# First norm's modulation: near halves as one-column TensorE products, far halves split over the engines

## The chip, the cores and the metric

The kernel runs on one core of a Trainium2 chip. The metric is device time of one execution in microseconds; the time of a kernel is the median of its runs. The engines are named as the profile does: PE (TensorE; PEld is its weight load), DVE (VectorE), ACT (ScalarE), POOL (GpSimd) and SP (SyncE, which issues nearly all DMAs).

## The reference, cut to what matters

```python
c_act = jax.nn.silu(c)
mod = c_act @ ada_w[l] + ada_b[l]                       # (1, 6*1024); ada_w is 1024 x 6144, f32
sh1, sc1, g1, sh2, sc2, g2 = [m[:, None, :] for m in jnp.split(mod, N_MOD, axis=-1)]
h = rmsnorm(x, norm_mix_w[l]) * (1.0 + sc1) + sh1       # x is 2048 x 1024
proj = h @ w_in[l]
...
x = x + g1 * mix
h = rmsnorm(x, norm_mlp_w[l]) * (1.0 + sc2) + sh2
```

Everything behind `proj` (a gated linear recurrence, sparse attention with a top-k indexer, a convolution module, the output product and a large MLP) fills the rest of the time; the change doesn't touch it. What it touches is the product of the vector `c_act` with the columns of `ada_w` that give `sc1` and `sh1`, 1024 columns each. No product with `w_in` can begin before the first columns of both are known.

## The kernel before

The sequence is cut into four blocks of 512 positions. For each block `in_block` normalizes x (`in_norm`), transposes it on PE into eight tiles of 128 channels, and applies scale and shift per channel while it splits each tile in a high part `ah` and a low part `al` (`to_act_steps`, L266: ACT makes `tf`, DVE makes `ah`, DVE or POOL makes `al`). Each unit of `w_in` then takes 24 PE products of 512 columns (three for each of eight channel tiles, `mm_T`, L357). Weights come in through SP's queue (`fetch_w`, `next_w`), are split by ACT (`whi`, L256) and POOL (`wlo`, L264), and the two parts are written back to DRAM for later blocks (`wk_d`).

Scale (`a1`) and shift (`sh1`) are made in four halves by `ada_half` (L207), 512 columns each, in this order: the first ("near") half of `a1` and of `sh1` at the kernel's start, L1677 and L1678, and the second ("far") halves in `first_units` (L1041), after the first two units have taken the products of channel tiles 0 to 3. Each half loads eight tiles `adw` of 128 rows x 512 columns, 256 KB each. Row tile k belongs to the column `cact[:, k]` of the activated c. For k = 1 and 2 ACT multiplies the tile by it (L224) and POOL adds the two (L227); for the other six DVE multiplies and accumulates (L229, L231). At the end `part_sum` sums the two folded tiles over the 128 partitions: PE takes 128 columns of the tile as stationary operand and a column of ones as moving operand, four such products for a tile, and each shows as two instructions (f32), all at L217. DVE then adds `ada_b` (L235) and, for `a1`, the norm's weight (L238).

The other four parts of the modulation come from `ada_gen` (L700), a side stream that the kernel pulls in small steps from the second block on: its parts (L183) load tiles of 128 x 256 (L186) into two buffers and accumulate on DVE (L188, L190).

The small constants (`ada_b`, the norms' weights and others) come as rows into the tile `rows` and are transposed once on PE to `cols` (L177, L178).

What sets the order: a scheduler works on a simulated time line when the program is built. It gives each engine its instructions in a fixed order, and takes first, of what is ready in its simulation, what stands earlier in the program; so work may run well ahead of its place in the program. Buffers belong to a pool and a tag, with a fixed number for each tag: "tf" (two buffers) holds the row of c, `rows`, the dumps of `in_norm`, and `tf` of `to_act_steps`. PSUM tiles go by tag as well. `S_st[h]` is the state of the recurrence of head h, which is cleared at the start and updated at the end of each head in each block (L680).

Of the kernel before, what the change touches and what calls it, by code (L numbers as in the profile page):

```python
# [8 lines left out]
F32 = mybir.dt.float32  # L9
# [7 lines left out]
OP = mybir.AluOpType  # L17
# [3 lines left out]
P = 128  # L21
D = 1024
L = 2048
TB = 512
NB = L // TB
NK = D // P
# [18 lines left out]
AK = [1, 2]  # L45
# [15 lines left out]
WQ, AQ, AB = 0, 0, 2  # L61
# [16 lines left out]
def trunk(ctx, tc, x, c, ada_w, ada_b, norm_mix_w, norm_mlp_w, w_in, hg_lb_logits,  # L78
# [3 lines left out]
    V, A, G, T = nc.vector, nc.scalar, nc.gpsimd, nc.tensor  # L82
# [11 lines left out]
    xp = ctx.enter_context(tc.tile_pool(name="xio", bufs=1))  # L94
# [19 lines left out]
    def ps_ax():  # L114
        return px["p"].tile([P, 512], F32, tag="ax", bufs=px["ax"], name=nm("ax"))
# [43 lines left out]
    pt = ps_ax()  # L159
# [13 lines left out]
        offs[key] = r0  # L173
        r0 += n
    cols = cst.tile([P, NROW], F32, name="cols")
    pt = ps_ax()
    T.transpose(pt[:, :NROW], rows, ident[:NROW, :NROW])  # L177
    V.tensor_copy(cols, pt[:, :NROW])  # L178

    def col(key, i=0, n=1):  # L180
        return cols[:, offs[key] + i:offs[key] + i + n]

    def ada_part(pool, wtag, wbufs, acc, sec, c0, w):  # L183
        for k in range(NK):
            t = pool.tile([P, w], F32, tag=wtag, bufs=wbufs, name=nm("adw"))
            (nc.gpsimd if AQ else nc.sync).dma_start(t, ada2[k * P:(k + 1) * P, sec * D + c0:sec * D + c0 + w])  # L186
            if k == 0:
                V.tensor_scalar(acc, t, cact[:, 0:1], None, op0=OP.mult)  # L188
            else:
                V.scalar_tensor_tensor(acc, t, cact[:, k:k + 1], acc, op0=OP.mult, op1=OP.add)  # L190
            yield 1.2 * w
# [12 lines left out]
    a2 = cst.tile([P, NK], F32, name="a2")  # L204
    g_d = {2: dram([1, D], F32, "g1_d"), 5: dram([1, D], F32, "g2_d")}

    def ada_half(sec, c0, dst, key, slots):  # L207
        acc = hp.tile([P, TB], F32, tag="cu", bufs=2, name=nm("adacc"))
        pt = ps_ax()
        n = TB // P  # L210
        t0 = c0 // P

        side = []

        def part_sum(t, vec, first, last):
            for i in range(n):
                T.matmul(pt[:, i:i + 1], t[:, i * P:(i + 1) * P], vec, start=(first and i == 0),  # L217
                         stop=last, skip_group_check=True)

        for k in range(NK):  # L220
            t = slots[k]()
            dma(t, ada2[k * P:(k + 1) * P, sec * D + c0:sec * D + c0 + TB])
            if k in AK:
                A.mul(t, t, cact[:, k:k + 1])  # L224
                side.append(t)
                if len(side) > 1:
                    G.tensor_tensor(side[0], side[0], t, OP.add)  # L227
            elif k == 0:
                V.tensor_scalar(acc, t, cact[:, 0:1], None, op0=OP.mult)  # L229
            else:  # L230
                V.scalar_tensor_tensor(acc, t, cact[:, k:k + 1], acc, op0=OP.mult, op1=OP.add)  # L231
        if side:
            part_sum(side[0], ones[:, 0:1], True, False)
        part_sum(acc, ones[:, 0:1], not side, True)
        V.tensor_tensor(dst[:, t0:t0 + n], pt[:, :n], col("adab", sec * 8 + t0, n), OP.add)  # L235
        if key is not None:
            part = slice(c0 // P, (c0 + TB) // P)
            V.scalar_tensor_tensor(dst[:, part], dst[:, part], 1.0, cols[:, offs[key] + part.start:offs[key] + part.stop],  # L238
                                   op0=OP.add, op1=OP.mult)
# [458 lines left out]
    AW = 256  # L698

    def ada_gen():  # L700
        for sec, dst in ((2, None), (4, a2), (3, sh2), (5, None)):
            for c0 in range(0, D, AW):
                acc = hp.tile([P, AW], F32, tag="ada", bufs=1, name=nm("adacc"))
                yield from ada_part(hp, "adw", AB, acc, sec, c0, AW)
                if dst is None:
                    pt = ps_xp(13)
                    T.matmul(pt[:1, :AW], ones, acc, start=True, stop=True)
                    row = hp.tile([1, AW], F32, tag="adw", bufs=AB, name=nm("adrow"))
                    dma(row, ada_b[0:1, sec * D + c0:sec * D + c0 + AW])
                    V.tensor_tensor(row, pt[0:1, :AW], row, OP.add)  # L710
                    dma(g_d[sec][:, c0:c0 + AW], row)
                else:
                    ada_col(acc, sec, c0, AW, dst)
            if sec == 4:
                ada_scale(a2, "nmlp")
# [325 lines left out]
    def first_units(xts):  # L1041
        act = [], []
        steps = to_act_steps(xts, a1, sh1, *act)
        ws = []
        for k in range(NK // 2):
            next(steps)
        for u in range(KO):
            ws.append(next_w())
            early.append(ps_at())
            mm_T(early[u], ws[u], act, True, None, 0, NK // 2)  # L1050
        ada_half(1, TB, a1, "nmix", far)
        ada_half(0, TB, sh1, None, far2)
        for _ in steps:
            pass
        for u in range(KO):
            mm_T(early[u], ws[u], act, True, None, NK // 2, NK)
        return act
# [616 lines left out]
    far2 = [slot("f", ZB), slot("k", ZB), slot("q", ZB), slot("v", VB), slot("gate", GB)]  # L1674
    far2 += [slot("at", 2), slot("at", 2), slot("u", 2)]
    xq = [in_norm(0)]
    ada_half(1, 0, a1, "nmix", near)  # L1677
    ada_half(0, 0, sh1, None, near)  # L1678
    while len(fetched) < NPF:
        sp = specs.pop(0)  # L1680
        fetched.append((fetch_w(*sp), sp))
# [73 lines left out]
```

## Time and profile before

| | us |
|---|---|
| median of 3 runs | 3005.93 |
| lowest, highest | 3005.49, 3018.01 |
| the profiled execution | 3011.41 |
| its span in the trace | 3009.7 |

The profile shows one execution, the profiled one; the other 1.7 us of its time lie around the span. All durations in this document are from that execution, while the comparison between kernels goes by the medians of runs. An engine's instructions run in their order; "idle before" a row is the time for which the engine stood, and the arrow names what ended it. PE's records of 512 columns overlap, so the distance of two starts, not the duration of one, is what a product costs in a stream.

### The profile page before, as it was taken

How to read it: one execution, taken by the hardware profiler on the slowest of the kernel's cores; microseconds unless marked ns; L12 is line 12 of the kernel's file. 1: busy time of each engine (PE TensorE's matmuls, PEld its weight loads, DVE VectorE, ACT ScalarE, POOL GpSimd, SP SyncE). 2: the span in 40 equal slices, each digit the busy share in tenths (PEclk: the TensorE clock that was granted, in tenths of full speed). 3: DMA queues.
4: the chain of work that ended last, by engine and by line, in shares of the span. 5: the costliest groups of instructions: out<-in, count | busy, mean ns of one | idle time of the engine just before them, and what ended most of it. 6: DMA issues, size and time to landing. Idle time of an engine off the chain costs nothing. (4 is left out here: it accounts for less than half of the span.)

```text
span 3009.7 us, 50821 instructions
## 1 busy us (share of the span) xinstructions
PE 2809.9 (93%) x18352; PEld 2539.2 (84%) x18352; DVE 1997.2 (66%) x3673; ACT 1545.7 (51%) x2885; POOL 1787.0 (59%) x1530
## 2 busy tenths in 40 slices
PE   6889989897999989999999999999989999989997
PEld 5768868786887888989898989998788899889997
DVE  7796486868437352766669566576988731487787
ACT  3436454445424235456566656466555544466654
POOL 7565152225305165566688666578766766867775
PEclk9999989998999999999999999999999999999999
DMA  8867756675665433444557545354899974465543
GB/s 265 275 195 249 222 175 219 197 216 187 202 195 168 137 121 129 120 127 140 148 165 228 155 137 148 100 179 153 256 295 313 305 237 141 147 207 178 178 124 110
DMA packets 479416, 560.10 MB, mean 186 GB/s; under 512 B 32615, under 2 KB 371884, under 8 KB 479148
## 3 DMA queue, kind: packets, MB, share of 16 engines
q1 hardware_dynamic: 478992, 556.65, 59.0%
q8 instruction: 145, 2.38, 0.3%
q14 instruction: 123, 1.01, 0.1%
q10 hardware_dynamic: 156, 0.07, 0.0%
HBM read 458.30 MB, written 98.31 MB: 185 GB/s over the span
## 5 line engine op out<-in xcount | busy, mean ns | idle before, releaser
L264 POOL TENSOR_TENSOR wlo<-wraw,whi 128x512 fp32r<-128x512 f32 x514 | 713.9, 1410 | 418.6 <-ACT whi L256 263.3
L256 ACT CAST whi<-wraw 128x1024 fp32r<-128x1024 f32 x257 | 269.7, 1050 | 335.8 <-PE ax L1172 105.8
L759 DVE SCALAR_TENSOR_TENSOR s<-r,iw_s,s 128x512 f32<-128x512 f32 (+3 forms) x266 | 267.3, 1005 | 193.6 <-ACT r L754 190.3
L357 PE MATMUL mm<-ah,wk 128*128 128x512 f32 x1104 | 296.9, 404 | 12.0 <-ACT k L577 3.3
L1172 PE MATMUL ax<-whi,hh 128*128 128x256 f32 x1600 | 278.9, 286 | 19.9 <-DVE acc L1334 13.1
L1172 PE MATMUL ax<-wlo,hh 128*128 128x256 f32 x1600 | 280.0, 285 | 0.0
L1172 PE MATMUL ax<-whi,hl 128*128 128x256 f32 x1600 | 275.8, 285 | 2.0 <-POOL hl L264 2.0
L941 POOL TENSOR_TENSOR pT<-L,pT 128x512 fp32r<-128x512 f32 (+3 forms) x160 | 201.5, 1261 | 123.7 <-ACT pT L940 104.7
L357 PE MATMUL mm<-ah,whi 128*128 128x512 f32 x936 | 256.4, 400 | 11.9 <-DVE gate L600 4.2
L357 PE MATMUL mm<-al,whi 128*128 128x512 f32 x936 | 257.1, 397 | 0.0
L1172 PEld LDWEIGHTS ax<-whi,hh 128*128 128x128 f32 x1600 | 232.1, 190 | 28.0 <-DVE acc L1334 12.9
L357 PEld LDWEIGHTS mm<-ah,wk 128*128 128x128 f32 x1104 | 207.2, 192 | 57.2 <-ACT k L577 4.0
L357 PE MATMUL mm<-ah,wlo 128*128 128x512 f32 x936 | 252.8, 394 | 0.0
L754 ACT ACTIVATE r<-ix 128x512 f32<-128x512 f32 (+3 forms) x256 | 141.4, 552 | 183.7 <-PE ix L752 177.3
L1172 PEld LDWEIGHTS ax<-wlo,hh 128*128 128x128 f32 x1600 | 232.2, 190 | 2.8
L1172 PEld LDWEIGHTS ax<-whi,hl 128*128 128x128 f32 x1600 | 229.7, 190 | 4.6 <-POOL hl L264 2.7
L528 POOL TENSOR_TENSOR cside<-cside,ctap 128x512 f32<-128x512 f32 x112 | 158.6, 1416 | 122.3 <-ACT ctap L527 105.8
L357 PEld LDWEIGHTS mm<-ah,whi 128*128 128x128 f32 x936 | 174.6, 191 | 49.5 <-DVE slo L470 4.9
L357 PEld LDWEIGHTS mm<-ah,wlo 128*128 128x128 f32 x936 | 175.2, 189 | 36.5
L357 PEld LDWEIGHTS mm<-al,whi 128*128 128x128 f32 x936 | 174.9, 190 | 35.1
L861 DVE TENSOR_SCALAR_CACHE_REDUCE cum<-s,ssm 128x384 bf16<-128x384 f32 (+13 forms) x112 | 165.3, 1475 | 6.5 <-POOL s L763 4.3
L1334 DVE TENSOR_TENSOR acc<-acc,ax 128x512 f32<-128x512 f32 x160 | 108.9, 682 | 84.9 <-PE ax L1172 84.5
(551 smaller groups left out, 6898.2 us busy)
## 6 DMA issues: line engine op xcount, KB each, us to landing
wraw<-in_mlp_w_dram SPq DMA_DIRECT2D x192, 512.0 KB, 4.1
wk<-wk_d SPq DMA_DIRECT2D x174, 512.0 KB, 4.9
kc<-sk_d SPq DMA_DIRECT2D x112, 256.0 KB, 3.8
vc<-v_d SPq DMA_DIRECT2D x112, 256.0 KB, 3.3
tsr<-in_mlp_w_dram SPq DMA_DIRECT2D x96, 256.0 KB, 5.8
ts_d<-tsr SPq DMA_DIRECT2D x48, 512.0 KB, 5.8
wr<-in_mlp_w_dram SPq DMA_DIRECT2D x96, 256.0 KB, 3.8
wr<-ts_d SPq DMA_DIRECT2D x72, 256.0 KB, 4.9
```

What stands on the lines that cost most here:

```text
L256: A.copy(hi, src)
L264: e.tensor_tensor(lo[:, i:j], src[:, i:j], hi[:, i:j].bitcast(F32), OP.subtract)
L357: T.matmul(ps, ww[:, k, :], aa[k], start=(n == 0 and k0 == 0), stop=(n == len(order) - 1 and k1 == NK))
L528: G.tensor_tensor(side, side, tap, OP.add)
L754: A.activation(r[:, :w], ps[:, :w], AF.Relu, scale=32.0 ** -0.5)
L759: V.scalar_tensor_tensor(s[:, c0:c0 + w], r[:, :w], iw, s[:, c0:c0 + w], op0=OP.mult, op1=OP.add)
L861: V.tensor_scalar(dump, s, t, -AIM - i * STEP, op0=OP.is_ge, op1=OP.add, accum_out=d)
L941: G.tensor_tensor(pT[:, :nt, 1], lv, pT[:, :nt, 0].bitcast(F32), OP.subtract)
L1172: T.matmul(ps[:, t * 256:(t + 1) * 256], aa[f][:, tok * P:(tok + 1) * P], ww[:, f, :], start=(first and n == 0 and (last or t == 0)), stop ...
L1334: V.tensor_tensor(dst, dst, src, OP.add)
```

## The change

All four halves are made by another division of the work. `ada_half` gets a list of row tiles (`on_pe`) whose product goes to PE directly: the tile's 128-column pieces are stationary and the moving operand is the column `cact[:, k]` itself, so that no other engine touches the tile. The near halves do this for all eight row tiles. The far halves do it for 5, 6 and 7; 1 and 2 stay with ACT and POOL, 0, 3 and 4 with DVE.

Three things go with it. The transpose that makes `cols` moves behind the products of the first half (`load_cols`). The far halves read a copy of `cact`, `cact2`, in a buffer of tag "tf". `ada_gen` reads another copy, `cact3`, into which a piece of `S_st[0]` is copied first, so that it can't be written before that state's update that precedes it in the program.

```diff
--- before.py
+++ after.py
@@ -173,14 +173,16 @@
         offs[key] = r0
         r0 += n
     cols = cst.tile([P, NROW], F32, name="cols")
-    pt = ps_ax()
-    T.transpose(pt[:, :NROW], rows, ident[:NROW, :NROW])
-    V.tensor_copy(cols, pt[:, :NROW])
+
+    def load_cols():
+        pt = ps_ax()
+        T.transpose(pt[:, :NROW], rows, ident[:NROW, :NROW])
+        V.tensor_copy(cols, pt[:, :NROW])
 
     def col(key, i=0, n=1):
         return cols[:, offs[key] + i:offs[key] + i + n]
 
-    def ada_part(pool, wtag, wbufs, acc, sec, c0, w):
+    def ada_part(pool, wtag, wbufs, acc, sec, c0, w, cact):
         for k in range(NK):
             t = pool.tile([P, w], F32, tag=wtag, bufs=wbufs, name=nm("adw"))
             (nc.gpsimd if AQ else nc.sync).dma_start(t, ada2[k * P:(k + 1) * P, sec * D + c0:sec * D + c0 + w])
@@ -204,34 +206,44 @@
     a2 = cst.tile([P, NK], F32, name="a2")
     g_d = {2: dram([1, D], F32, "g1_d"), 5: dram([1, D], F32, "g2_d")}
 
-    def ada_half(sec, c0, dst, key, slots):
+    def ada_half(sec, c0, dst, key, slots, on_pe, cact):
+
         acc = hp.tile([P, TB], F32, tag="cu", bufs=2, name=nm("adacc"))
         pt = ps_ax()
         n = TB // P
         t0 = c0 // P
 
-        side = []
-
-        def part_sum(t, vec, first, last):
+        side, vec = [], []
+        begun = []
+
+        def part_sum(t, v, last):
             for i in range(n):
-                T.matmul(pt[:, i:i + 1], t[:, i * P:(i + 1) * P], vec, start=(first and i == 0),
+                T.matmul(pt[:, i:i + 1], t[:, i * P:(i + 1) * P], v, start=(not begun),
                          stop=last, skip_group_check=True)
+                begun.append(i)
 
         for k in range(NK):
             t = slots[k]()
             dma(t, ada2[k * P:(k + 1) * P, sec * D + c0:sec * D + c0 + TB])
-            if k in AK:
-                A.mul(t, t, cact[:, k:k + 1])
+            cv = cact[:, k:k + 1]
+            if k in on_pe:
+                part_sum(t, cv, len(on_pe) == NK and k == NK - 1)
+            elif k in AK:
+                A.mul(t, t, cv)
                 side.append(t)
                 if len(side) > 1:
                     G.tensor_tensor(side[0], side[0], t, OP.add)
-            elif k == 0:
-                V.tensor_scalar(acc, t, cact[:, 0:1], None, op0=OP.mult)
+            elif not vec:
+                V.tensor_scalar(acc, t, cv, None, op0=OP.mult)
+                vec.append(k)
             else:
-                V.scalar_tensor_tensor(acc, t, cact[:, k:k + 1], acc, op0=OP.mult, op1=OP.add)
+                V.scalar_tensor_tensor(acc, t, cv, acc, op0=OP.mult, op1=OP.add)
         if side:
-            part_sum(side[0], ones[:, 0:1], True, False)
-        part_sum(acc, ones[:, 0:1], not side, True)
+            part_sum(side[0], ones[:, 0:1], False)
+        if vec:
+            part_sum(acc, ones[:, 0:1], True)
+        if (sec, c0) == (1, 0):
+            load_cols()
         V.tensor_tensor(dst[:, t0:t0 + n], pt[:, :n], col("adab", sec * 8 + t0, n), OP.add)
         if key is not None:
             part = slice(c0 // P, (c0 + TB) // P)
@@ -698,10 +710,14 @@
     AW = 256
 
     def ada_gen():
+
+        cact3 = hp.tile([P, 8], F32, tag="cact3", bufs=1, name="cact3")
+        V.tensor_copy(cact3, S_st[0][:, :8])
+        V.tensor_copy(cact3, cact)
         for sec, dst in ((2, None), (4, a2), (3, sh2), (5, None)):
             for c0 in range(0, D, AW):
                 acc = hp.tile([P, AW], F32, tag="ada", bufs=1, name=nm("adacc"))
-                yield from ada_part(hp, "adw", AB, acc, sec, c0, AW)
+                yield from ada_part(hp, "adw", AB, acc, sec, c0, AW, cact3)
                 if dst is None:
                     pt = ps_xp(13)
                     T.matmul(pt[:1, :AW], ones, acc, start=True, stop=True)
@@ -1048,8 +1064,11 @@
             ws.append(next_w())
             early.append(ps_at())
             mm_T(early[u], ws[u], act, True, None, 0, NK // 2)
-        ada_half(1, TB, a1, "nmix", far)
-        ada_half(0, TB, sh1, None, far2)
+
+        cact2 = xp.tile([P, 8], F32, tag="tf", bufs=2, name="cact2")
+        V.tensor_copy(cact2, cact)
+        ada_half(1, TB, a1, "nmix", far, (5, 6, 7), cact2)
+        ada_half(0, TB, sh1, None, far2, (5, 6, 7), cact2)
         for _ in steps:
             pass
         for u in range(KO):
@@ -1674,8 +1693,8 @@
     far2 = [slot("f", ZB), slot("k", ZB), slot("q", ZB), slot("v", VB), slot("gate", GB)]
     far2 += [slot("at", 2), slot("at", 2), slot("u", 2)]
     xq = [in_norm(0)]
-    ada_half(1, 0, a1, "nmix", near)
-    ada_half(0, 0, sh1, None, near)
+    ada_half(1, 0, a1, "nmix", near, range(NK), cact)
+    ada_half(0, 0, sh1, None, near, range(NK), cact)
     while len(fetched) < NPF:
         sp = specs.pop(0)
         fetched.append((fetch_w(*sp), sp))
```

## Rows read from the trace of the kernel before

**Rows 1.** The page: the span, and part 1, busy time of each engine with its share of the span and its number of instructions.

```profile
span 3009.7 us, 50821 instructions
...
PE 2809.9 (93%) x18352; PEld 2539.2 (84%) x18352; DVE 1997.2 (66%) x3673; ACT 1545.7 (51%) x2885; POOL 1787.0 (59%) x1530
```

**Rows 2.** Windows of the start, of all engines. Columns: stretch and its length, then for PE, its weight loads, DVE, ACT and POOL the busy us with the number of instructions, the granted clock of PE, the busy share of the DMA engines and GB/s.

```profile
0.00:20.00 20.00, 3.88 (x15) 2.73 (x15) 9.64 (x31) 9.53 (x16) 15.94 (x25) 1.00 0.84 287
20.00:25.00 5.00, 4.65 (x20) 4.14 (x20) 4.93 (x12) 0.42 (x1) 3.11 (x3) 1.00 1.07 219
```

**Rows 3.** Timeline of PE, 7 to 50 us. Columns: start, us that the merged group takes, engine, line, operation, output<-inputs, stationary rows*columns, shapes, count; in brackets the idle time before it and what ended that.

```profile
14.66 1.87 PE L217 MATMUL ax<-ones,adw 128*128 128x1 f32 x8 [2.66 <-POOL adw L227]
...
20.00 1.87 PE L217 MATMUL ax<-ones,adacc 128*128 128x1 f32 x8 [0.36 <-DVE adacc L231]
...
21.72 1.09 PE L272 MATMUL mm<-ident,xt 128*128 128x128 f32 x4
...
23.16 1.87 PE L217 MATMUL ax<-ones,adw 128*128 128x1 f32 x8 [0.35 <-POOL adw L227]
...
36.35 0.80 PE L357 MATMUL at<-al,whi 128*128 128x512 f32 x1 [0.90 <-POOL al L282]
...
39.93 0.63 PE L357 MATMUL at<-al,whi 128*128 128x512 f32 x1
...
42.44 0.95 PE L217 MATMUL ax<-ones,adw 128*128 128x1 f32 x8
...
43.56 0.39 PE L357 MATMUL at<-ah,wlo 128*128 128x512 f32 x1
...
46.44 1.03 PE L217 MATMUL ax<-ones,adw 128*128 128x1 f32 x8
```

**Rows 4.** Timeline of DVE, 5 to 72 us, same columns.

```profile
10.36 0.49 DVE L229 TENSOR_SCALAR adacc<-adw,cact 128x512 f32<-128x512 f32 x1 [3.15 <-DMA adw<-in_ada_w_dram]
...
30.11 0.16 DVE L235 TENSOR_TENSOR sh<-ax,cols 128x4 f32<-128x4 f32 x1 [0.82 <-PE ax L217]
...
48.56 0.35 DVE L188 TENSOR_SCALAR adacc<-adw,cact 128x256 f32<-128x256 f32 x1
...
48.94 0.48 DVE L190 SCALAR_TENSOR_TENSOR adacc<-adw,cact,adacc 128x256 f32<-128x256 f32 x1
...
49.42 0.16 DVE L405 CAST sconst<-sint 128x14 f32<-128x14 int32 x1
...
50.60 0.16 DVE L235 TENSOR_TENSOR sh<-ax,cols 128x4 f32<-128x4 f32 x1
```

**Rows 5.** Timeline of ACT, 5 to 82 us.

```profile
30.36 1.45 ACT L277 ACTIVATE tf<-mm,sh,a 128x512 f32<-128x512 f32 x2 [1.27 <-DVE sh L235]
...
76.25 1.04 ACT L256 CAST whi<-wraw 128x1024 fp32r<-128x1024 f32 x1 [9.78 <-DMA wraw<-in_w_in_dram]
```

**Rows 6.** Timeline of POOL, from the start to 50 us.

```profile
1.04 0.14 POOL L404 IOTA sint<- 128x14 int32 x1
...
34.59 1.71 POOL L282 TENSOR_TENSOR al<-tf,ah 128x512 fp32r<-128x512 f32 x1
```

**Rows 7.** Windows of PE alone, one us each. Columns: stretch and length, busy us with the number of instructions, granted clock, DMA share, GB/s.

```profile
47.00:48.00 1.00, 0.47 (x5) 1.00 0.36 127
48.00:49.00 1.00, 0.30 (x2) 0.61 0.08 33
```

**Rows 8.** Timeline of PE, 40 to 62 us.

```profile
48.70 1.87 PE L217 MATMUL ax<-ones,adacc 128*128 128x1 f32 x8 [1.23 <-DVE adacc L231]
...
52.54 0.80 PE L357 MATMUL at<-ah,whi 128*128 128x512 f32 x1 [1.97 <-DVE ah L281]
...
58.26 0.50 PE L357 MATMUL at<-ah,wlo 128*128 128x512 f32 x1
```

**Rows 9.** Timeline of PE, 553 to 562 us (the second block): the stretch that follows a wait, with no idle time shown from its first row on. L272 and L661 are transposes, L553 are one-column products.

```profile
553.39 1.11 PE L272 MATMUL mm<-ident,xt 128*128 128x128 f32 x4 [0.89 <-DVE ah L281]
...
554.72 0.43 PE L553 MATMUL ax<-ones,cu 128*128 128x1 f32 x2
...
556.61 1.09 PE L272 MATMUL mm<-ident,xt 128*128 128x128 f32 x4
```

**Rows 10.** Windows of PE alone in that stretch, columns as in rows 7.

```profile
556.00:557.00 1.00, 1.00 (x6) 0.50 0.23 68
557.00:558.00 1.00, 1.00 (x7) 0.50 0.23 72
```

**Rows 11.** Timeline of SP's queue (issues of DMAs), from the start to 130 us.

```profile
63.47 3.96 SPq L186 DMA_DIRECT2D adw<-in_ada_w_dram  x2
...
70.05 0.38 SPq L106 DMA_DIRECT2D wraw<-in_w_in_dram  x1
```

**Rows 12.** Timeline of PE, 60 to 90 us.

```profile
78.55 3.46 PE L357 MATMUL mm<-ah,whi 128*128 128x512 f32 x8 [3.39 <-DVE slo L470]
```

**Rows 13.** The instructions that write or read the tiles `adw`, up to 60 us: count, then ns least/median/most, first and last start in us, form.

```profile
L231 DVE SCALAR_TENSOR_TENSOR adacc<-adw,cact,adacc x20: 627/752/1780, 12.7 to 47.9; 128x512 f32<-128x512 f32 x20
...
L224 ACT ACTIVATE adw<-adw,cact x8: 706/716/722, 11.3 to 39.6; 128x512 f32<-128x512 f32 x8
...
L227 POOL TENSOR_TENSOR adw<-adw,adw x4: 1680/1725/1746, 12.9 to 43.2; 128x512 f32<-128x512 f32 x4
```

**Rows 14.** The instructions on the tiles `S_st`, whole span, same columns.

```profile
L680 DVE SCALAR_TENSOR_TENSOR S_st<-sa,fb,ax x16: 327/346/347, 186.5 to 1113.9; 128x128 f32<-128x128 f32 x16
```

## The prediction

> **What bounds the kernel now.** I read the page first: one profiled execution with a span of 3009.7 us, TensorE (PE) busy in 93% of it [rows 1]. Over the whole run PE is the bound, but the change touches only the first 50 us and a side stream (`ada_gen`). So the question is local: how long does PE stand between the start and its dense products, and what ends those waits? I went on to the windows of the start, then to the order of instructions on PE, then to VectorE (DVE), ScalarE (ACT) and GpSimd (POOL), each over the same stretch.
>
> The start has three steps. (1) Sixteen near tiles of `ada_w` and four of x are loaded; the first of the sixteen is used at 10.36 us [rows 4]. The DMA windows give 287 GB/s x 20 us = 5.74 MB by 20 us and 219 GB/s after it [rows 2]; x (2.1 MB) and the near tiles (4.2 MB) make 6.3 MB, so the last near tile is there at about 23 us at the earliest. (2) DVE, ACT and POOL fold each half into one or two tiles, PE sums these over the partitions, and at 30.11 us the first half of `sh1` is made [rows 4]; the first activation with it starts at 30.36 [rows 5]. (3) The same again for the second halves, among the first 24 products of the first two units. DVE's long run of L231 is what PE waits for last: 1.23 us ahead of the eight products at 48.70 [rows 8]. The second `sh1` comes at 50.60 [rows 4]. In all of this PE stands waiting for sums that others make, and is not the bound of the start. That is what the change alters.
>
> **The clock in the start.** PE's price is the whole case, so I read it from durations, since the clock column is 1.00 there from the beginning [rows 2] and tells nothing before its first change. Eight one-column products (four of `part_sum`; each is two instructions) take 1.87 us at 14.66 and at 20.00, but 0.95 at 42.44; a 512-column product takes 0.63 us at 39.93 and 0.39 at 43.56 [rows 3]. So PE runs at the lower level (1.2 GHz) until about 41 us and at 2.4 GHz after it. Start to start, one instruction of a one-column product costs 1.78/8 = 0.222 us at the low level (20.00 to 21.72 holds eight of them) and 0.119 at the high one. Would a long stream of them raise the clock? Three places say no. From 20.00 to the end of the work at 23.16 PE is nearly without a gap in them and in transposes [rows 2, 3], and it is still slow afterwards. From 553.39 to 557.5 it is busy without a gap in the same two kinds of work [rows 9], and the windows inside and behind that stay at 0.50 [rows 10]. At 48.2 us the clock falls, after a stretch in which one-column products had just taken over from dense ones and only some 0.7 us after the last of these ended [rows 3, 7]. I take the low level for the near halves.
>
> **Term A, the near halves, on the path.** Removed: per half six DVE operations (L231 median 0.752 us, [rows 13]), two ACT multiplies of 0.716 and a POOL addition of 1.725 [rows 13], all beside other work. Added: every tile goes to PE, 16 tiles x 8 instructions x 0.222 = 28.5 us, against 32 such instructions before. Tiles arrive faster (16 by 23 us) than PE takes them (1.78 us each), so PE is busy from 10.36 to 10.36 + 28.5 = 38.9 us whatever the DMAs do. PE also has eight transposes of x for k = 0 and 1, four in 1.09 us [rows 3]; with no idle PE time left they add 2.2 us on one side or the other of the sums. With 0.4 us for the last addition and the activation's start, the step that began at 30.36 begins at 38.9 + 2.2 + 0.4 = 41.5: **A = +11.1 us**. Bounds: +8.9 (transposes in gaps that I don't see) to +11.1. The work taken off DVE, ACT and POOL is worth nothing there, since PE is later than all three. `load_cols` moves the transpose of `cols` behind the first half (0.39 us on PE in either place); its first reader would be the scale at about 25 us, and PE comes no earlier. It costs nothing.
>
> The Trainium skill puts a weight load much lower: "TensorE: Matmul & The Clock Gate", section "LDWEIGHTS (loading the stationary operand)", gives columns/1.2 ns, 107 ns for 128 columns. By it the near halves would need some 14 us of PE, an estimate, and would end with the DMA. The trace does not agree: 0.222 us per load and product at the low level. It is the third rival below.
>
> **Term B, from there to the end of the first two units.** `cact2` lies in a "tf" buffer, of which there are two. Buffers of a tag go out in program order: `sconst` ("cu") had its input from 1.04 us on [rows 6] and was first written at 49.42 [rows 4], behind the last `adacc`. So `cact2` is written when the low part of k = 2 has freed a buffer, some 6.5 us after step A (0.7 for ACT, 0.8 for DVE, 1.3 to 1.7 for POOL, twice). Behind it wait all second-half products, on ACT, DVE and PE. On PE the second halves have (3 + 1 + 1) x 8 x 2 = 80 instructions instead of 32: 48 more, 5.7 us at 0.119, 10.7 at 0.222. Dense products run among them, so I take the high level for two thirds: 32 x 0.119 + 16 x 0.222 = 7.4. What goes: DVE has 3 operations per half instead of 6, so its 1.23 us wait [rows 8] falls away, and the 0.90 us wait for the low part at 36.35 [rows 3] too, because POOL had been busy with the weights' low parts until 34.59 [rows 6] and is now long free. **B = +7.4 - 2.1 = +5.3 us.** Lower bound: all at the high level and no fall, which also spares the nine products (0.2 us each) and eight transposes (0.1 each) that ran slow between 52.54 and 58.26 [rows 8]: 5.7 - 2.1 - 2.6 = +1.0. Upper bound: all 48 at 0.222 and the 26 of the 48 dense products that now run fast slow as well (26 x 0.2): +15.8.
>
> **Term C, the side stream.** `ada_gen` is from the second block on, yet today its first DMAs and DVE operations run ahead into the start: L188 and L190 at 48.56 and 48.94 [rows 4], and an L186 that occupies SP's queue for 3.96 us from 63.47 [rows 11], behind which the weight load of 70.05 stands. That load is what ACT waits 9.78 us for [rows 5], and PE then idles 3.39 us before 78.55 [rows 12]. `cact3` reads `S_st[0]` after its first update, not before 186.5 us [rows 14], so all but the first two DMAs, which need only free buffers, go behind it. Behind the copy itself nothing waits: this state is next written a block later. I take **C = -3 us**; bounds -3.4 (all of PE's gap) and 0 (the weights' own buffers were not free earlier).
>
> **Term D, the rest.** The nine L188/L190 operations that ran early (5.7 us) now run between 350 and 780 us, where DVE has idle time; PE waits for none of them. Every later order on the engines is made anew. I take 0, with -3 to +5.7.
>
> Sum: 11.1 + 5.3 - 3 + 0 = **+13.4 us**. Against the profiled execution (3011.41 us with what lies around the span) that is 3024.8; the median before is 3005.93, 5.5 us below that execution, and on it I get **3019 us** (+0.45%). About 0.5%, 15 us, is what a measurement of this kernel can tell from no change. Ends of all terms: 8.9 + 1.0 - 3.4 - 3 = +3.5, and 11.1 + 15.8 + 0 + 5.7 = +32.6.
>
> **The rivals.**
> 1. The clock stays low through the first units (slower by over 0.5%). Place: from step A to the end of the second halves; PE has 80 slow instructions there, and the fall at 48.2 us shows that they don't hold the clock. Price: B at its upper end, 11.1 + 15.8 - 3 = +23.9, 3030 us. It decides from the point where over half of the 80 run in one stretch. Against it: the dense products at 43 us did raise the clock. 0.22.
> 2. The delay is taken up later: PE's gaps after 60 us (3.39 us at 78.55) end on weight loads that need not move with the start, so that part of A and B vanishes there; A + B halved, less 3: +5, 3011 us. For it: the DMA share is near 1 in the start. Against: those loads hang on buffers that PE itself frees. 0.13.
> 3. The near products cost half, by the high clock or a cheaper load. Then step A ends with the DMA, at 23 + 1 + 0.4 = 24.4 instead of 30.36; POOL's weight parts (to 34.59) hold the first products, so only 4 of the 6 us arrive; with B at +1 and C at -3 that is -6, 3000 us. Against it are rows 3, 9 and 10. 0.08.
> 4. The buffer doesn't hold `cact2` back, and the 80 instructions stand ahead of the first activation, all at the low level: 17.8 instead of 7.4, +24, 3030 us. Against it: `sconst`. 0.04.
>
> **How the numbers follow.** Forecast 0.53, about three fifths of it below +15 us. Slower by over 0.5%: 0.21 + 0.20 + 0.03, 0.43 with a little taken off for a luckier order. Faster by over 0.5% (below 2991) needs rival 3 and a better order on top: 0.05. The rest, 0.52, is within. Range: the low end takes in rival 2 and half of rival 3 (3002); the high end rivals 1 and 4 with some of D (3033).
>
> **What would show it.** Right: one-column products on PE without a gap from about 10.4 to 39 us, eight in 1.78 us; first L277-type activation at 39 to 42 us; second `sh1` at 62 to 69; no L188/L190 before 186 us; the idle before the fourth unit shorter than 3.39 us. Wrong: eight products in under 1.2 us before 35 us, an activation before 32 us, or a difference that arises after 100 us.

## The result and the profile after

The changed kernel takes 3041.72 us (median of 5 runs, 3039.62 to 3048.37) against 3006.18 for the kernel before on the same chip (5 runs, 3005.49 to 3018.01): a ratio of 1.0113 [1.0094, 1.0132], +35.5 us. The forecast was +13.4 us, 3019, with a range up to 3033. The sign of the sum holds, its size does not. All ratios here leave out four slow executions of 3128 to 6937 us (one each of `o1`, `r2`, `r3` and of the kernel before in the same series). The profiled execution has this page (part 1: busy us, share of the span, instructions):

```profile
span 3040.0 us, 51084 instructions
...
PE 2848.7 (94%) x18496; PEld 2577.6 (85%) x18496; DVE 1964.2 (65%) x3658; ACT 1535.1 (50%) x2877; POOL 1779.1 (59%) x1528
```

Against [rows 1] PE has 144 instructions more (96 of the near halves, 48 of the far ones); DVE, ACT and POOL have fewer.

**The start.** The timeline of PE (columns as in rows 3; line numbers are shifted: L221 is the one-column product, L284 the transposes of x, L369 `mm_T`):

```profile
10.23 13.79 PE L221 MATMUL ax<-cact,adw 128*128 128x1 f32 x64 [6.85 <-DMA adw<-in_ada_w_dram]
...
24.05 13.73 PE L221 MATMUL ax<-cact,adw 128*128 128x1 f32 x64
37.64 1.95 PE L284 MATMUL mm<-ident,xt 128*128 128x128 f32 x8
...
44.83 0.55 PE L369 MATMUL at<-ah,whi 128*128 128x512 f32 x1
45.21 0.40 PE L369 MATMUL at<-al,whi 128*128 128x512 f32 x1
...
50.69 2.51 PE L221 MATMUL ax<-cact,adw 128*128 128x1 f32 x22
...
54.84 4.77 PE L221 MATMUL ax<-cact,adw 128*128 128x1 f32 x24
59.47 1.84 PE L221 MATMUL ax<-ones,adw 128*128 128x1 f32 x8
61.18 1.85 PE L221 MATMUL ax<-ones,adacc 128*128 128x1 f32 x8
...
89.16 1.98 PE L369 MATMUL mm<-ah,whi 128*128 128x512 f32 x8
```

PE is in one-column products without a gap from 10.23 to 37.8 us (but for the 0.37 us transpose of `cols`), at 13.79/64 = 0.215 us each. The clock is at the low level (1.2 GHz) to about 45 us (a 512-column product falls from 0.55 to 0.40 us there), high (2.4 GHz) among the first far products (22 in 2.51 us) and low again for the last 40 of them (24 in 4.77 us, 8 in 1.84). The unit that begins at 89.16 no longer waits for DVE as it did at 78.55 [rows 12]; the prediction calls it the fourth, but 96 products of 512 columns stand before it, so it is the fifth. On ACT the first activation, on DVE the copy of `cact2` (L1069) and the second `sh1` (L247):

```profile
39.68 1.45 ACT L289 ACTIVATE tf<-mm,sh,a 128x512 f32<-128x512 f32 x2 [10.60 <-PE mm L284]
```

```profile
45.70 0.17 DVE L1069 COPY cact<-cact 128x8 f32<-128x8 f32 x1 [1.39 <-POOL al L294]
...
63.06 0.16 DVE L247 TENSOR_TENSOR sh<-ax,cols 128x4 f32<-128x4 f32 x1 [1.01 <-PE ax L221]
```

First activation 39.68 against 30.36 [rows 5], second `sh1` 63.06 against 50.60 [rows 4]. `ada_gen`'s first DVE operation comes at 205 us.

**Behind the start.** The 4512 512-column products of `mm_T` are the same in every kernel here, so their starts are a clock for the program's progress. Product n is the one that n others precede. The changed kernel is 9.3 us late at product 0, 10.6 at product 96 (the start of the fifth unit), 11.5 at 192 (117 us in the kernel before), 14.1 at 768, 27.7 at 2304 (1150 us) and 30.3 at the end of the span. So a third of the loss arises in the start and half of it between products 192 and 2304, where nothing was edited but the side stream, which `cact3` holds back to there. That stretch in windows of PE, the kernel after and then before (columns: stretch, its length, busy us with instructions, granted clock, DMA share, GB/s):

```profile
128.50:1177.80 1049.30, 952.57 (x5651) 0.93 0.59 190
```

```profile
117.00:1150.10 1033.10, 940.51 (x5653) 0.95 0.60 192
```

The number of instructions is the same to two; PE is busy 12.1 us longer with them and waits 4.1 us longer. Counted by the granted clock's changes, PE runs 136.5 us of it at the low level in 20 falls, against 99.0 us in 16. Work takes about twice as long at the low level (eight wide products 3.76 against 1.98 us, below and above), so that 37.5 us more of it would cost half, 19 us, if PE worked all through it; the busy time shows 12. The mean granted clock of whole runs goes the same way: 0.966 to 0.970 in the five runs of the changed kernel, 0.970 to 0.976 in 65 runs of the kernel before beside the experiments.

The waits of PE there, after and then before (engine, line, what it waited for: us in total, times, longest):

```profile
PE ax L659 <- DVE k L617: 21.2, 11, 5.8
PE ax L651 <- DVE k L617: 12.4, 9, 3.0
PE mm L369 <- ACT k L589: 6.9, 4, 4.8
PE ax L651 <- DVE q L616: 6.6, 2, 3.4
```

```profile
PE ax L647 <- DVE k L605: 20.5, 9, 4.4
PE ax L639 <- DVE k L605: 11.0, 7, 4.8
PE ax L661 <- DVE k L605: 10.4, 3, 4.7
```

The kind is the same (PE waits for DVE's scaling of q and k in the recurrence), and so is the sum: all waits for the scaled q and k are 40.5 us after and 41.9 before. Which steps wait, and how often, is not the same. One place where time is lost, first on PE after, then on DVE after:

```profile
406.29 1.33 PE L651 MATMUL ax<-q,k 128*128 128x64 f32 x8 [3.39 <-DVE q L616]
407.38 3.47 PE L369 MATMUL mm<-ah,wk 128*128 128x512 f32 x8
...
414.82 1.97 PE L651 MATMUL ax<-q,k 128*128 128x64 f32 x8 [2.96 <-DVE k L617]
416.55 3.76 PE L369 MATMUL mm<-ah,wk 128*128 128x512 f32 x8
```

```profile
399.01 1.81 DVE L542 SCALAR_TENSOR_TENSOR cacc<-hc,cvc,cacc 128x512 f32<-128x512 f32 x1
400.75 0.74 DVE L630 TENSOR_TENSOR at<-ax,ident 128x256 f32<-128x256 f32 x2
401.41 0.85 DVE L634 TENSOR_TENSOR q<-q,f 128x512 f32<-128x512 f32 x1
402.18 1.50 DVE L617 TENSOR_TENSOR k<-k,f 128x256 f32<-128x256 f32 x1
403.60 0.47 DVE L192 SCALAR_TENSOR_TENSOR adacc<-adw,cact,adacc 128x256 f32<-128x256 f32 x1
404.00 0.74 DVE L542 SCALAR_TENSOR_TENSOR cacc<-hc,cvc,cacc 128x512 f32<-128x512 f32 x1
404.66 0.71 DVE L632 COPY_PREDICATED at<-lmask,ax 128x128 f32<-128x128 uint8 x2
405.17 0.97 DVE L616 TENSOR_TENSOR q<-q,f 128x256 f32<-128x256 f32 x1
```

DVE has no gap here (busy all 22 us from 398 to 420): two steps of the convolution (L542) and one of the side stream (L192) stand ahead of q in its order. PE waits 3.39 us for the q at 405.17, and its next eight wide products take 3.47 us where eight at the high level take 1.98. The same step of the recurrence, counted by its products, in the kernel before, first on DVE, then on PE:

```profile
368.89 0.68 DVE L622 TENSOR_TENSOR q<-q,f 128x512 f32<-128x512 f32 x1
...
370.69 0.46 DVE L604 TENSOR_TENSOR q<-q,f 128x256 f32<-128x256 f32 x1
```

```profile
375.36 0.78 PE L639 MATMUL ax<-q,k 128*128 128x64 f32 x6
...
394.65 3.78 PE L357 MATMUL mm<-ah,wk 128*128 128x512 f32 x8 [3.04 <-ACT k L577]
```

No step of the convolution stands between there, q is ready 4.2 us ahead of PE, and PE doesn't wait. Across this place the changed kernel's lateness grows from 15.6 us (product 806) to 20.6 (product 809). Its second wait, at 414.82, costs nothing against the kernel before, which waits 3.04 us for ACT and runs as slowly behind it at the same products (394.65): the lateness is 21.6 us ahead of them and 21.9 behind.

### The profile page after: what moved, and what is told of

The parts are those of the page before. It is cut to its first block, busy times and chain, and to the rows that moved or that the text cites. A ratio compares the mean times of both kernels' runs of the same rounds, so it can differ in the third digit from the quotient of the medians.

```text
span 3040.0 us, 51084 instructions
## 1 busy us (share of the span) xinstructions
PE 2848.7 (94%) x18496; PEld 2577.6 (85%) x18496; DVE 1964.2 (65%) x3658; ACT 1535.1 (50%) x2877; POOL 1779.1 (59%) x1528
## 5 line engine op out<-in xcount | busy, mean ns | idle before, releaser
L369 PE MATMUL mm<-ah,wk 128*128 128x512 f32 x1104 | 299.3, 406 | 6.1 <-ACT k L589 2.2
L369 PE MATMUL mm<-ah,whi 128*128 128x512 f32 x936 | 261.3, 405 | 10.2 <-ACT k L589 4.8
L1191 PEld LDWEIGHTS ax<-whi,hh 128*128 128x128 f32 x1600 | 234.1, 192 | 28.2 <-DVE acc L1353 12.5
L369 PE MATMUL mm<-ah,wlo 128*128 128x512 f32 x936 | 254.6, 396 | 0.0
L369 PE MATMUL mm<-al,whi 128*128 128x512 f32 x936 | 254.6, 396 | 0.0
L369 PEld LDWEIGHTS mm<-ah,wk 128*128 128x128 f32 x1104 | 208.6, 194 | 50.8 <-ACT k L589 2.9
L369 PEld LDWEIGHTS mm<-ah,whi 128*128 128x128 f32 x936 | 177.7, 194 | 48.3 <-ACT k L589 5.1
L369 PEld LDWEIGHTS mm<-ah,wlo 128*128 128x128 f32 x936 | 175.5, 190 | 36.4
L369 PEld LDWEIGHTS mm<-al,whi 128*128 128x128 f32 x936 | 175.1, 190 | 35.5
```

What stands on the lines that cost most here:

```text
L369: T.matmul(ps, ww[:, k, :], aa[k], start=(n == 0 and k0 == 0), stop=(n == len(order) - 1 and k1 == NK))
L1191: T.matmul(ps[:, t * 256:(t + 1) * 256], aa[f][:, tok * P:(tok + 1) * P], ww[:, f, :], start=(first and n == 0 and (last or t == 0)), stop ...
```

## The experiments

The theories, by the letters of the recorded expectations. S: `cact3` costs the later loss, since it moves the side stream. L: the late start itself costs again in the middle. O: the order of the instructions on PE and DVE behind the start, made anew for each kernel, costs it. D (in `r2`): the other division of the near work does. The table has for each kernel its ratio, how late its 512-column product n starts against the profiled execution of before, then the stretch from product 192 to 2304: length, PE's idle time, time at the low clock and falls of the clock. Ratios come from 4 to 10 runs of each kernel and 5 to 25 of the kernel before on the same chip, the other columns from one profiled execution, and such single executions lie up to 11 us off their kernel's median (`o2`, `r1` and `r3` 8 to 11 below). The last column is the ratio's gap in us less the lateness at product 192: what the time loses behind the start. One quarter of a per cent is 7.5 us; by the intervals the last column is good to about 4 to 6 us, to 8 to 10 for `e1`, `e3` and `q1`.

```
kernel            ratio [95%]               n=0    48    96   192  2304  stretch  idle   low falls  rest
before                                        0     0     0     0     0   1033.1  92.6  99.0  16      0
after             1.0113 [1.0094, 1.0132]   9.3  12.6  10.6  11.5  27.7   1049.3  96.7 136.5  20     22
e1_no_cact3       1.0107 [1.0074, 1.0141]  11.3  18.2  17.3  17.8  34.8   1050.1  99.0 136.5  18     14
e2_cact3_alone    0.9993 [0.9979, 1.0007]   0.4  -1.0  -4.6  -4.5   3.3   1041.0  94.3 119.5  19      2
e3_near_alone     1.0090 [1.0059, 1.0120]  13.7   5.4   3.0   4.3  27.0   1055.8 106.7 129.7  18     23
e4_far_alone      1.0062 [1.0042, 1.0081]   0.3   9.5   8.7   6.9  24.8   1051.0  94.2 133.1  22     12
o1_before_fast940 0.9997 [0.9985, 1.0009]   1.8   1.7   3.5   3.2   0.4   1030.3  86.0  95.6  15     -4
o2_before_ada760  1.0057 [1.0040, 1.0074]   0.9   0.6   0.5  -0.3  13.7   1047.2  96.5 122.9  20     17
o3_before_at1560  1.0009 [0.9996, 1.0021]   0.3   0.3   0.3   1.5   2.6   1034.2  85.0 122.9  22      1
o4_after_fast940  1.0122 [1.0105, 1.0139]   9.8  16.7  14.0  17.1  38.8   1054.8 102.2 133.1  20     20
p1_after_ada760   1.0096 [1.0079, 1.0113]   9.6  13.3  11.4  13.3  30.0   1049.8  99.3 129.7  19     16
p2_after_at1560   1.0116 [1.0099, 1.0132]   9.7  13.1  11.2  15.4  36.9   1054.6 100.3 136.5  22     20
p3_after_tk1250   1.0132 [1.0115, 1.0149]   9.6  16.1  14.7  15.6  37.7   1055.3 100.7 126.3  21     24
p4_near_split     1.0065 [1.0048, 1.0082]   7.3   4.0   3.6   5.7  26.3   1053.7 102.2 126.3  21     14
r1_late_four      1.0015 [0.9998, 1.0031]  12.7   1.2  -2.3  -2.7  -1.2   1034.5  91.5 105.8  18      7
r2_near_127       1.0016 [0.9999, 1.0032]   0.7  -1.9  -2.3  -3.2   6.2   1042.6  97.6 112.6  19      8
r3_near_34567     1.0031 [1.0016, 1.0046]  11.8   2.4  -1.2  -1.5   4.8   1039.5  91.3 109.2  20     11
q1_before_three   1.0077 [1.0049, 1.0105]   0.6   0.5   0.6   1.9  14.3   1045.5  91.7 119.5  20     21
```

The expectations of `p1` to `p4` name a marker read from windows (1062.1 us before, 1074.5 after); the table and the last runs count the products themselves (1033.1 and 1049.3).

**The parts, one by one.** `e1` takes `cact3` out of the change; `e2` is the kernel before with `cact3` and `load_cols` alone; `e3` has the near halves alone, `e4` the far halves with `cact2` alone, both without `cact3`.

```diff
e2:  +  load_cols() behind the first half; cact3 and its two copies; ada_part(..., cact3)
e1:  -        cact3 = ...; two copies      -  ada_part(..., cact3)   +  ada_part(..., cact)
e3:  -  ada_half(..., far, (5, 6, 7), cact2)    +  ada_half(..., far, (), cact)
e4:  -  ada_half(..., near, range(NK), cact)    +  ada_half(..., near, (), cact)
```

> The changed kernel, but ada_gen reads cact itself as before; near and far halves as changed. The changed kernel is 35.5 us slower than before: about 10.5 us are there at 100 us, about 20 arise between 150 and 1000 us. Theory S (side stream): the 20 us come from cact3, which moves the start of ada_gen; then this gives the loss of the start alone, and without the relief of the weight load at 70 us, some 3017 to 3021 us. Theory O (order): the later 20 us come from the instruction order behind the start being made anew, whatever the edit, so that the clock of TensorE falls more often; then nothing points to cact3, and this may land anywhere from 3013 to 3045, with its later loss in other places than the changed kernel has it.

> The kernel before with ada_gen reading cact3, and load_cols behind the first half; near and far halves divided as before. Theory S: the start is no later (3 us earlier by the weight load), and the 20 us of the middle are all there: 3020 to 3026 us, with the loss between 150 and 1000 us. Theory O: the start as before, the middle somewhere between 3 us better and 20 us worse, 3000 to 3026, not tied to the side stream.

> The near halves on TensorE for all eight row tiles (and load_cols); far halves divided as before without cact2, ada_gen reads cact as before. Both theories: first activation at 39 to 41 us instead of 30.4, so +9 to +11 us at 100 us. Theory S: nothing further, 3015 to 3018 us. Theory O: 3010 to 3040, a later difference in either direction. A third view, that the products of the near halves are fast (high clock), would give an activation before 32 us.

> The far halves divided over four engines with cact2 (and load_cols); near halves as before, ada_gen reads cact as before. The first activation stays at about 30.4 us. The 48 more one-column instructions cost 5.7 to 10.7 us on TensorE, 2 us of waits go: second half of sh1 at 52 to 58 us instead of 50.6, so +1 to +8 us at 100 us. Theory S: nothing further, 3007 to 3014 us. Theory O: 3000 to 3035.

S falls: `e2` costs nothing that can be measured, and `e1` loses as much as the whole change. But `cact3` is worth 6.7 us in the start of the changed kernel (17.3 to 10.6 at product 96), 5.6 of them by product 48; in `e1` a step of the side stream waits 3.44 us on DVE for its tile, ahead of the first `ah`. `e3` says that the near halves alone are late by 13.7 us at product 0 and by 3.0 at product 96: the second halves go on beside them and are ready at 56.69 us, 6.1 us later than before. `e4` says that the far halves hold what they cost. Its two `sh1` on DVE, and PE between them:

```profile
30.41 0.16 DVE L247 TENSOR_TENSOR sh<-ax,cols 128x4 f32<-128x4 f32 x1 [1.61 <-PE ax L221]
...
59.42 0.16 DVE L247 TENSOR_TENSOR sh<-ax,cols 128x4 f32<-128x4 f32 x1 [0.58 <-PE ax L221]
```

```profile
45.76 1.84 PE L221 MATMUL ax<-cact,adw 128*128 128x1 f32 x16
47.46 1.68 PE L221 MATMUL ax<-ones,adw 128*128 128x1 f32 x8
49.00 1.85 PE L221 MATMUL ax<-ones,adacc 128*128 128x1 f32 x8
50.71 5.26 PE L221 MATMUL ax<-cact,adw 128*128 128x1 f32 x24
```

PE passes from the high level (16 in 1.84 us) to the low one (8 in 1.85) and stays there; 56 of the 80 run so, and the second `sh1` is 8.8 us later than before. Both parts alone lose more behind the start (23 and 12 us) than in it; `e3` does so though it is only 4.3 us late at product 192.

**Only the order.** The order of each engine's instructions comes from a schedule in the program with assumed rates. These kernels shift one assumed rate (three in `q1`) and compute the same with the same instructions. How much of the order of before is left can be counted in the traces, where an instruction is known by its line, tiles and shapes. Of the neighbouring pairs on DVE, by tenths of its instructions, the changed kernel keeps 0.35 to 0.47 from the second to the fourth tenth, `o1` 0.38 to 0.64, `q1` 0.33 to 0.63, `o2` 0.38 to 0.92 and `o3` 0.46 to 0.78; from the sixth tenth on (some 1300 us) all keep 0.98 or more.

```diff
o1, o4:  -FAST = 979                    +FAST = 940       (o1 of before, o4 of after)
o2, p1:  -"ada": 800.0                  +"ada": 760.0     (o2 of before, p1 of after)
o3, p2:  -R1 = [1126, 1216, 1594]       +R1 = [1126, 1216, 1560]
p3:      -R1 = [1126, 1216, 1594]       +R1 = [1126, 1250, 1594]
q1:      the three of o1, o2 and o3 together, of before
```

> The kernel before with one number of its side work changed: FAST 940 instead of 979, the credit that the recurrence's queue gets at each step. No work is added or removed, the start (to 70 us) keeps its order, and the order of instructions on the engines changes behind it about as much as in the changed kernel. Theory O (the loss behind the start comes from the order being made anew, any order but this one costs more waits and more falls of the clock): +8 to +25 us against before, with 20 to 40 us more at the lower clock between 70 and 1150 us. Theory L (a late start itself is what costs in the middle, because weights, side work and TensorE then meet in other ways): within 5 us of before, since the start is not late.

> The kernel before with the credit of ada_gen at 760 instead of 800 a step; otherwise as before, start in the same order. Theory O: +5 to +25 us against before, the sign the same as for the other shifts. Theory L: within 5 us of before.

> The kernel before with the credit of the attention queue at 1560 instead of 1594 in the first stage; otherwise as before, start in the same order. Theory O: +5 to +25 us against before. Theory L: within 5 us of before.

> The changed kernel with FAST 940 instead of 979: the same late start (10 to 13 us behind before at 80 us), another order behind it. Theory O: the part behind the start is drawn anew, so the time moves by up to 15 us in either direction from the changed kernel (3025 to 3055 by the first median of before). Theory L: the late start is the same and so is its cost, within 5 us of the changed kernel.

> The changed kernel with the credit of ada_gen at 760 instead of 800: same start, the order behind it drawn anew. From the 81st 512-column product of the first kind to the 2321st the changed kernel takes 1074.5 us, before 1062.1. Theory O (this stretch depends on the order alone, and a late start says nothing about it): between 1060 and 1083, and over the three shifts p1 to p3 at least one below 1068. Theory L (every order behind the late start loses 10 us or more there): all three at 1072 or more.

> The changed kernel with the attention queue's credit at 1560 instead of 1594: same start, other order behind it. Theory O: the stretch takes 1060 to 1083 us, one of p1 to p3 below 1068; time as the start's 11 us plus that. Theory L: 1072 us or more in all three.

> The changed kernel with the top-k queue's credit at 1250 instead of 1216: same start, other order behind it. Theory O: the stretch takes 1060 to 1083 us, one of p1 to p3 below 1068. Theory L: 1072 us or more in all three.

> The kernel before with three numbers of the side work changed at once (FAST 940, ada_gen 760, attention 1560): start as before, the order behind it as far from before's as the changed kernel's is. If the order of before is simply better than nearly every other one, the stretch takes 1045 to 1056 us and the kernel 10 to 22 us more than before, though its start is untouched. If an untouched start keeps the middle good, 1030 to 1042 us.

`o2` and `q1` lose 17 and 21 us behind a start that is the old one to 2 us: the order alone can cost what the change lost there. The windows of `q1` over the stretch, columns as above:

```profile
118.90:1164.40 1045.50, 953.78 (x5653) 0.94 0.60 190
```

PE's idle time is that of before (91.7 us); its busy time is 13.3 us longer with the same instructions, at a lower clock (0.968 to 0.972 over its four whole runs). So in this execution the loss is in the clock and not in the sum of the waits; that the place of the waits decides what the clock does is argued, not shown. Time at the low clock alone doesn't settle it either: `o3` has 122.9 us of it, more than `q1`, and loses nothing, since it waits 8 us less. `o1` too loses nothing, with an order about as far from before's as `q1`'s. My expectation that one of `p1` to `p3` would recover most of the loss missed: all four orders drawn anew behind the changed start lose 16 to 24 us. That is what L forecast for them, and for `o1` and `o3` too; O was right for `o2`, `q1` and, below, `p4`.

**Lateness without a new division.** `r1` keeps the division of the kernel before and adds, in each near half, 16 one-column products (32 instructions) whose results nobody reads, so that the first activation is as late as in the changed kernel. `p4`, `r2` and `r3` give the near halves other divisions, with far halves and side stream as before.

```diff
r1, in ada_half:
+        if slots is near:
+            for _ in range(4):
+                for i in range(n):
+                    T.matmul(pt[:, 8 + i:9 + i], acc[:, i * P:(i + 1) * P], ones[:, 0:1], ...)
p4:  near on_pe = (5, 6, 7)     r2:  near on_pe = (1, 2, 7)     r3:  near on_pe = (3, 4, 5, 6, 7)
```

> Near halves as the changed kernel divides the far ones: row tiles 5, 6 and 7 to TensorE directly, 1 and 2 to ScalarE and GpSimd, 0, 3 and 4 to VectorE; far halves and ada_gen as before. If the near step of the changed kernel is bound by TensorE at 0.215 us for each one-column instruction, then 80 of them instead of 128 take 17.2 us from the first tile at 10.3 us, so the first activation comes at 28 to 32 us, not at 39.7, and the start is within 3 us of before. If it is bound by the DMAs or by another engine, it stays late. The order behind it is another one again: theory O 1060 to 1083 us in the stretch, theory L 1060 to 1066, since the start isn't late.

> The kernel before with 4 x 4 more one-column products at the end of each near half, into PSUM columns that nobody reads: TensorE is held up by some 7 us per half, the division of the work is as before. Behind the start its instruction order is that of e2_cact3_alone, which took 1041.0 us from product 192 to product 2304. Theory O (order alone): 1039 to 1043 us in the stretch, however late the start; in all e2's time plus the lateness, which is 8 to 15 us at product 192. Theory L (a late start costs again in the middle): 1049 us or more.

> Near halves with row tiles 1, 2 and 7 to TensorE and the other five to VectorE, nothing for ScalarE and GpSimd; far halves and ada_gen as before. Its instruction order behind the start is that of before. Theory O: 1031 to 1035 us from product 192 to 2304, and in all before plus what the start changes there (-3 to +4 us). Theory D (the other division of the near work is what costs in the middle): 1049 us or more, as in the other kernels with a divided near half.

> Near halves with row tiles 3 to 7 to TensorE, 1 and 2 to ScalarE and GpSimd, 0 to VectorE; far halves and ada_gen as before. Its instruction order behind the start is that of e4_far_alone, whose stretch took 1051.0 us with the near halves untouched. Theory O: 1049 to 1053 us, the same as e4_far_alone although another part of the start is changed. 112 one-column instructions in the near halves: first activation between 34 and 39 us.

The ACT timeline of `r1`:

```profile
40.19 1.45 ACT L282 ACTIVATE tf<-mm,sh,a 128x512 f32<-128x512 f32 x2 [3.84 <-PE mm L277]
```

A first activation at 40.19 us instead of 30.36 is caught up by product 96 (-2.3 us) and costs the time 0.15%, with an interval that holds zero (the stretch is 1.4 us longer, in the fastest of its ten executions). So a late first activation doesn't cost by itself. But `r1`, made to be late, is not late behind product 96, and no kernel here has the changed kernel's 11.5 us at product 192 together with the order of before: L is not needed for a loss (`o2`, `q1`), and it is not excluded for the changed kernel. `p4` missed its place (first activation 37.67, expected 28 to 32) and still is early enough at product 96; its loss is behind it, 14 us. Kernels that share an order behind the start (0.97 or more of the pairs on DVE from the second tenth on) lose alike there by their ratios: `e4` and `r3` 12 and 11 us, `after` and `e1` 22 and 14, `before` and `r2` 0 and 8, `e2` and `r1` 2 and 7. D is not borne out by `r2`, whose 8 us are good to 5. The profiled executions of such pairs agree less: their stretches are 1051.0 and 1039.5, 1033.1 and 1042.6, 1041.0 and 1034.5 us, so the forecasts for the stretch of `r1`, `r2` and `r3` all missed, by 5 to 10 us. Differences of that size in one execution's stretch, busy or low-clock time, the 12.4 us of `q1`'s stretch among them, carry little; the last column carries the argument.

## Why the prediction was wrong, point by point

**Term A: right, 1.8 us too large.** 0.215 us for each one-column instruction (0.222 forecast), no gap, low level to the end, the eight transposes behind them, first activation 39.7 instead of 41.5 (+9.3, forecast +11.1). It is on the path because the second halves begin behind it, with `cact2`; where they are made beside the near halves, mostly on DVE (`e3`), A leaves 3.0 us at product 96.

**Term B: mis-sized, within its bounds.** The far halves begin with `cact2` behind the "tf" buffer (DVE 45.70, 6 us behind the first activation, as said). From the first activation to the second `sh1` it is 23.4 us, 20.2 before: +3.1 us, forecast +5.3. The forecast took two thirds of the 48 more instructions at the high level; of all 80, 40 ran at the low one. Alone (`e4`) 56 of them did, and the far halves cost 8.7 us at product 96. Together A and B put the second `sh1` 12.5 us later, forecast 16.4.

**Term C: the wait found, the size missed.** In the changed kernel 2.0 us come back from product 48 to 96 (12.6 to 10.6), forecast 3, and the wait of [rows 12] is gone. But against `e1`, without `cact3`, the relief is 6.7 us, beyond the bound of 3.4, and most of it is there before the weight load that the prediction looked at.

**A + B + C** gave 10.6 us at product 96 against 13.4, in the forecast's order of steps. That it comes so near is partly luck: without `cact3`, A and B are 17.3 us there (`e1`; 16.4 forecast), and C makes up more than it was given.

**Term D: the step that failed.** "Every later order on the engines is made anew. I take 0, with -3 to +5.7." Measured: by the profiled executions 16 us from product 192 to 2304 and 3 behind it, by the medians about 24 us behind product 192 (22 by the ratio). The bound of 5.7 was the work that moved (nine DVE operations of the side stream, which runs from 205 us and not from 350), when the thing at stake was the place of all other DVE steps among each other. DVE has idle time in the span's mean (66% busy), and that is what I read; from 398 to 420 us of the changed kernel it has none, and there its order decides when PE waits. In the stretch PE's waits grew by 4 us and its busy time, at a lower clock, by 12. The prediction had listed "a difference that arises after 100 us" as what would make it wrong, and gave it no chance of its own.

**The rivals.** The clock (1): partly true; it was high from 45.2 us, and low again for 40 of the 80. Delay taken up later (2): not in the changed kernel, which is 12.6, 10.6 and 11.5 us late at products 48, 96 and 192; near halves alone (`e3`) do catch up, but by product 48 and not on weight loads. Cheap products (3): refuted, the near products took 27.5 us. By the Trainium skill's "TensorE: Matmul & The Clock Gate", section "LDWEIGHTS (loading the stationary operand)", a load of 128 columns takes 107 ns, which would give some 14 us, an estimate; the trace does not agree. `cact2` not held back (4): refuted by 45.70.

**What stays open.** That a new order can cost 17 to 21 us with nothing else changed is shown (`o2`, `q1`). That it is the order, and not the lateness or `cact3`, that costs the changed kernel its 22 us is argued: it rests on `e1`, `e2` and the pairs that share an order; the old order behind the new start was not tried. All eight new orders drawn behind a changed division of the halves (those of `after`, `e3`, `e4`, `o4`, `p1` to `p4`) lose 11 to 24 us. Of the five others that were drawn (`o1`, `o2`, `o3`, `q1`, `e2`) two lose 17 to 21 and three -4 to 2. Why is not settled, and it leaves room for a part of the lateness beside the draw. No kernel tried is shown to be faster than the one before.

## What to carry to other kernels

Where one schedule with assumed rates orders all engines, a local edit costs its local sum plus a new draw of the order everywhere behind it: here -4 to +24 us by kernel, twice what the edit itself cost at the most. Give that draw a term of its own, sized by a few kernels that shift one assumed number and change nothing else, and test an edit against a control that shares its order. A step that is ready later is on the path only if what follows it could not have been made meanwhile; look for the readiness that the next stage waits for last.

## What the runs showed of the hardware that was not expected

27.5 us of one-column products, with no gap but one small transpose, left PE at the low level; among the 512-column products that followed from 42.12 us on it came up (0.40 us each from 45.21), and among the next one-column products, from 54.84 us, it was low again (granted clock 0.50 from 57 to 69 us). In the middle of the kernel the same 5653 instructions kept PE busy 940.5 us in one order and 953.8 in another (`q1`), with equal idle time and the clock low for 99.0 and 119.5 us. Part of that is scatter of single executions: with the order of before, `r2` kept PE busy 944.9 us.
